# Running sum of the convolution in a PSUM bank, low parts of the projection weights on GpSimd

## The chip, the cores and the metric

One core of one Trainium2 chip runs the program. The metric is the time of one execution on the device in microseconds (us), median over runs. The core has TensorE (PE in the profile; PEld is its weight load), VectorE (DVE), ScalarE (ACT), GpSimd (POOL) and SyncE (SP), which issues the DMAs here. Each engine takes its instructions from its own queue, strictly in order.

## The reference, cut to what matters

One decoder layer over 1024 tokens and 1024 features:

```
u    = rmsnorm(x, norm_g) * (1 + scale) + shift        # scale, shift, gate from c
proj = u @ w_in                                        # 1024 -> 7168 columns
a    = conv_a * sigmoid(conv_bp)
a    = causal_depthwise_conv(a, conv_w, conv_b)        # 31 taps per channel
a    = silu(layernorm(a)) @ conv_pw
y_conv = a * silu(conv_gate)
r    = retention(rotary(q), rotary(k), v)              # 4 heads, in chunks
y_ret  = head_groupnorm(r) * silu(ret_gate)
h    = x + gate * (concat(y_conv, y_ret) @ w_out)
out  = rmsnorm(h, final_g)
```

## The kernel before, in words

Every big product is made three times over, to keep float32 precision: each operand is split into a high part (`hi`, a cast on ScalarE) and a low part (`lo`, the operand minus its high part, a subtraction on VectorE), and `mm3` (L70) adds hi·hi, hi·lo and lo·hi in PSUM.

A **unit** (L75) is 128 columns of a weight matrix times the resident 1024 x 1024 operand: two PSUM tiles of 128 x 512 (`ps[0]`, `ps[1]`, one bank each), for each of eight k three matmuls into `ps[0]` and three into `ps[1]`, 48 in all. `load_w` (L61) fetches a unit's weights (128 x 1024), casts the high part on ScalarE and makes the low part on VectorE; `raw`, `hi` and `lo` have two buffers each. The PSUM tiles of the units come from the pool `mm` with four banks (L48), so that two units can be in PSUM at once. The other four banks belong to the head of the kernel, later to the retention (`tr`, `sp`, `op`, `up`), at the end to the layer norm.

The stages, in order of time:

1. The head (until about 65 us): x is normalised and turned, `u` is built k by k, and four units (`EARLY`) run along with it.
2. Projection, convolution and retention (until about 700 us). `conv_pair(m)` (L250) makes a tile of 128 channels: a unit whose result goes through a sigmoid, a second unit whose PSUM result VectorE multiplies by it into the tile `a` (L260; 30 zero columns, set by GpSimd at L256, stand ahead of it). There are two buffers for `a`: pair m can write its `a` only once the taps of pair m - 2 are done. `conv_taps` (L233) then makes 31 taps on VectorE over 128 x 1024, each adding into the SBUF tile `y`, and adds `y` to `ysum` (L244). The taps have a priority 3000 below the rest, so they fill the time that VectorE has left. For each of four heads: `rotary` twice for q and k (units read out of PSUM by ScalarE, or twice by VectorE, L322 and L324), `values` (L329, weights of two `load_w` at once), two gate units, and `retention` in four chunks, in which GpSimd makes a power (`pow`, L422) for the group norm. `conv_pair` and `conv_gate` stand between these.
3. From `ysum` a matmul makes the mean (`mu`, L496); the layer norm of the convolution, the last gates, the output projection of the retention half, the pointwise convolution, the output projection of the convolution half and the final norm follow, with the low parts on VectorE through `split` (L57).

The order of the instructions in each engine's queue isn't written out by hand: a scheduler lays the program out on a timeline of its own, taking at each step the ready instruction of the highest priority, and that order is then fixed.

Of the kernel before, what the change touches and what calls it, by code (L numbers as in the profile page):

```python
# [12 lines left out]
P = 128  # L13
S = 1024
# [10 lines left out]
HALF = 512  # L25
EARLY = (8, 0, 9, 1)  # the units that run while u is built

# columns of the packed per-channel vectors
V_C, V_SH, V_SC, V_NG, V_CB, V_LG, V_LB, V_GG, V_GB, V_CW = 0, 8, 16, 24, 32, 40, 48, 56, 64, 72
V_N = V_CW + KT * CW  # L30
# columns of the packed decay constants
K_G, K_G2, K_KD = 0, 2 * H, 4 * H
# [6 lines left out]
def hybrid_layer(ctx: ExitStack, tc: tile.TileContext, x, vec, c_row, ada_ss, ada_g, adab_g, w_e, w_m, w_v,  # L39
# [7 lines left out]
    dram = ctx.enter_context(tc.tile_pool(name="dram", bufs=1, space=bass.MemoryType.DRAM))  # L47
    mmp = ctx.enter_context(tc.tile_pool(name="mm", bufs=4, space=bass.MemoryType.PSUM))  # L48

# [5 lines left out]

# [1 line left out]
    def split(hi, lo, src):  # L57
        nc.scalar.copy(hi, src)  # L58
        nc.vector.tensor_tensor(lo, src, hi.bitcast(F32), op=SUB)  # L59

    def load_w(src, shape, name, pool=None):  # L61
        raw = wpool.tile(shape, F32, tag="raw", name=f"raw_{name}")
        nc.sync.dma_start(raw, src)
        pool = pool or wpool
        hi = pool.tile(shape, F32R, tag="hi", name=f"hi_{name}", bufs=2)
        lo = pool.tile(shape, F32R, tag="lo", name=f"lo_{name}", bufs=2)
        split(hi, lo, raw)
        return hi, lo
# [6 lines left out]
    def unit(wh, wl, rh, rl, name, halves_first=False, pool=None, tag="mm"):  # L75
        """[128 columns of w]^T times the resident operand, both halves of its free axis."""
        ps = [(pool or mmp).tile([P, HALF], F32, tag=tag, name=f"ps_{name}_{i}") for i in range(2)]
        order = [(k, i) for k in range(KT) for i in range(2)]
        if halves_first:
            order.sort(key=lambda o: o[1])  # L80
        for k, i in order:
            sl = slice(i * HALF, (i + 1) * HALF)
            mm3(ps[i], wh[:, k], wl[:, k], rh[k][:, sl], rl[k][:, sl], k == 0, k == KT - 1)
        return ps

# [1 line left out]
    vec_t = const.tile([P, V_N], F32, name="vec_t")  # L87
# [11 lines left out]
    def col(base, k):  # L99
        return vec_t[:, base + k:base + k + 1]  # L100

    def bcast_rsqrt(pool, psp, sums, scale, n, rb):
        """sums: [128, n] column sums (token t = 128 j + partition); rb: PSUM [128, 128 n] gets rsqrt in every row."""
        v = pool.tile([P, n], F32, tag="rs_v", name="rs_v")
        nc.vector.tensor_scalar(v, sums, scale, EPS, op0=MUL, op1=ADD)
        r = pool.tile([P, n], F32, tag="rs_r", name="rs_r")
        nc.gpsimd.tensor_tensor(r, v, mhalf[:, :n], op=ALU.pow)
        for j in range(n):
            dg = pool.tile([P, P], F32, tag="rs_d", name="rs_d", bufs=4)
            nc.vector.tensor_scalar(dg, ident_t, r[:, j:j + 1], None, op0=MUL)  # L110
            nc.tensor.matmul(rb[:, j * P:(j + 1) * P], ones_t, dg, start=True, stop=True)

# [1 line left out]
    xts = [big.tile([P, D], F32, tag="big", name=f"xt{t}", bufs=17) for t in range(TT)]  # L114
# [10 lines left out]
    def head():  # L125
        """Builds u tile by tile and runs the first four units along with it, k on the outside."""
        xs = hp.tile([P, KT, S], F32, name="xs")
# [25 lines left out]
        def norm(t, xt_):  # L153
            """x / rms(x) of 128 tokens, turned so that features are on partitions."""
            ms = hp.tile([P, 1], F32, tag="ms", name=f"ms{t}", bufs=3)
            nc.scalar.activation(junk2, xt_, AF.Square, scale=D ** -0.5, accum_out=ms)
            nc.gpsimd.tensor_scalar(ms, ms, EPS, None, op0=ADD)
            nc.gpsimd.tensor_tensor(ms, ms, mhalf[:, 0:1], op=ALU.pow)
            nc.vector.tensor_scalar(xt_, xt_, ms, None, op0=MUL)
            for q in range(2):  # L160
                tp = hps.tile([P, 4, P], F32, tag=("paa", "pbb", "pcc", "pdd")[(2 * t + q) % 4], name=f"xp{t}{q}")
                for j in range(4):
                    k = 4 * q + j
                    nc.tensor.transpose(tp[:, j], xt_[:, k * P:(k + 1) * P], ident_t)
                dst = xs[:, 4 * q:4 * q + 4, t * P:(t + 1) * P]
                if q == 0 and t < 7:
                    nc.scalar.copy(dst, tp)
                else:
                    nc.vector.tensor_copy(dst, tp)
# [42 lines left out]
        make_u(0, halves(1))  # L212
        ps = [[mmp.tile([P, HALF], F32, tag="mm", name=f"ps_e{n}{i}") for i in range(2)] for n in range(2)]
        ps += [[hps.tile([P, HALF], F32, tag=t, name=f"ps_{t}") for t in u] for u in (("pcc", "pbb"), ("paa", "pdd"))]
# [18 lines left out]
    def conv_taps(m, ap):  # L233
        """Convolves one tile of channels; fills whatever time the vector engine has left."""
        with tc.high_priority(offset=-TAPS_LATER):
            y = convp.tile([P, S], F32, tag="y", name=f"y{m}")
            nc.vector.tensor_scalar(y, ap[:, 0:S], col(V_CW, m * CW), col(V_CB, m), op0=MUL, op1=ADD)
            for j in range(1, CW):
                nc.vector.scalar_tensor_tensor(y, ap[:, j:j + S], col(V_CW, m * CW + j), y, op0=MUL, op1=ADD)  # L239
            nc.sync.dma_start(d_y[m], y)  # L240
            if m == 0:
                nc.vector.tensor_copy(ysum, y)
            else:
                nc.vector.tensor_tensor(ysum, ysum, y, op=ADD)  # L244

    def in_unit(n):
        wh, wl = load_w(w_m[n - sum(e < n for e in EARLY)], [P, KT, P], f"w{n}")
        return unit(wh, wl, uh, ul, f"w{n}")
# [29 lines left out]
    def out_gate():  # L278
        """One step towards the residual's gate, the same in every partition."""
        k = len(gate_steps)  # L280
# [20 lines left out]

# [1 line left out]
    with tc.tile_pool(name="ret", bufs=1, reuse_waits="tile") as rp, \  # L303
# [25 lines left out]
        def values(h):  # L329
            vt = rp.tile([P, TT, 2 * P], F32, tag="v", name=f"v{h}")  # L330
            ws = [load_w(w_v[h, g], [P, 4, 2 * P], f"v{h}{g}") for g in range(2)]
            for tg in range(2):
                ps = [mmp.tile([P, 2, 2 * P], F32, tag="mm", name=f"ps_v{h}{tg}{i}") for i in range(2)]
                for k in range(KT):
                    wh, wl = ws[k // 4]
                    for j in range(4):
                        sl = slice((4 * tg + j) * P, (4 * tg + j + 1) * P)
                        mm3(ps[j // 2][:, j % 2], uh[k][:, sl], ul[k][:, sl], wh[:, k % 4], wl[:, k % 4],
                            k == 0 and j % 2 == 0, k == KT - 1 and j % 2 == 1)
                for i in range(2):  # L340
                    nc.scalar.copy(vt[:, 4 * tg + 2 * i:4 * tg + 2 * i + 2], ps[i])
            return vt

        def retention(h, q, k, v, sg):
            state = st_h = st_l = None
            for c in range(NCH):
# [10 lines left out]
                if c < NCH - 1:  # L357
                    # keys with tokens on partitions, decayed to the chunk's end
                    kth = rp.tile([P, 2, 2 * P], F32R, tag="kth", name=f"kth{n}")
# [12 lines left out]

                # scores, transposed: keys on partitions
                sp = rps.tile([P, 3 * P], F32, tag="sp", name=f"sp{n}")
# [10 lines left out]

                # outputs, tokens on partitions
                op = rps.tile([P, 2, 2 * P], F32, tag="op", name=f"op{n}")
# [23 lines left out]

                # group norm over the head's 256 values
                st6 = rp.tile([P, 2, 6], F32, tag="st6", name=f"st6{n}", bufs=2)
# [62 lines left out]
        negmu = f2.tile([P, S], F32, tag="y1", name="negmu")  # L476
        # layer norm, channels on partitions; what fits in before u is gone comes first
        def ln_center(m, tmp):
# [22 lines left out]

# [1 line left out]
    with tc.tile_pool(name="fin", bufs=1, reuse_waits="tile") as fp, \  # L503
# [62 lines left out]

# [1 line left out]
        for m in range(KT):  # L568
# [14 lines left out]

# [1 line left out]
        for t in range(TT):  # L585
# [48 lines left out]
def _layout(inp):  # L634
# [27 lines left out]

    # tables that depend on the shapes alone
    f4 = np.float32
# [52 lines left out]
```

## Time and profile before

| | |
|---|---|
| time, median of 2 runs | 1003.42 us (1003.21 to 1003.64) |
| span of the profiled execution | 1001.6 us |
| PE busy | 987.8 us, 99% |
| DVE busy | 739.3 us, 74% |
| ACT busy | 312.8 us, 31% |
| POOL busy | 35.9 us, 4% |

The span runs from the first to the last instruction of the profiled execution; the time of this execution itself isn't given apart from the two runs, which lie 1.6 to 2.0 us above the span. A busy time is what the engine worked; matmuls are pipelined, so a busy PE is not PE at its peak.

### The profile page before, as it was taken

How to read it: one execution, taken by the hardware profiler on the slowest of the kernel's cores; microseconds unless marked ns; L12 is line 12 of the kernel's file. 1: busy time of each engine (PE TensorE's matmuls, PEld its weight loads, DVE VectorE, ACT ScalarE, POOL GpSimd, SP SyncE). 2: the span in 40 equal slices, each digit the busy share in tenths (PEclk: the TensorE clock that was granted, in tenths of full speed). 3: DMA queues.
4: the chain of work that ended last, by engine and by line, in shares of the span. 5: the costliest groups of instructions: out<-in, count | busy, mean ns of one | idle time of the engine just before them, and what ended most of it. 6: DMA issues, size and time to landing. Idle time of an engine off the chain costs nothing.

```text
span 1001.6 us, 12564 instructions
## 1 busy us (share of the span) xinstructions
PE 987.8 (99%) x5108; PEld 843.6 (84%) x5108; DVE 739.3 (74%) x969; ACT 312.8 (31%) x489; POOL 35.9 (4%) x55
## 2 busy tenths in 40 slices
PE   7999999999999999999999999999999999999997
PEld 5888899888898888899888898888888888888886
DVE  6959999899998999999967679764446963442342
ACT  7831223332213322223233412443422711111221
POOL 2000000000000000100000000000000000000000
PEclk9999999999999999999999999999999999999999
DMA  9641111111132211113221022411784356541322
GB/s 351 236 168 43 43 43 64 63 64 43 64 106 74 74 63 63 43 64 127 63 84 42 25 103 63 147 64 64 264 277 152 127 172 209 187 137 63 127 95 84
DMA packets 40253, 108.80 MB, mean 109 GB/s; under 512 B 3458, under 2 KB 16002, under 8 KB 39043
## 3 DMA queue, kind: packets, MB, share of 16 engines
q1 hardware_dynamic: 40050, 107.74, 31.5%
q8 instruction: 40, 0.66, 0.3%
q10 hardware_dynamic: 144, 0.26, 0.1%
q14 instruction: 19, 0.15, 0.0%
HBM read 84.92 MB, written 23.07 MB: 108 GB/s over the span
## 4 chain that ended last, share of the span: by engine, by line
PE 96%; DVE 1%; DMA 1%; ACT 0%; issue 0%; SPq 0%; POOL 0%; POOLq 0%; DVEq 0%; ACTq 0%
PE ps_w L73 16%; PE ps_w L71 16%; PE ps_w L72 16%; PE ps_v L71 3%; PE ps_v L73 3%; PE ps_v L72 3%; PE ps_oc L73 3%; PE ps_or L72 3%; PE ps_oc L72 3%; PE ps_oc L71 3%; PE ps_or L73 3%; PE ps_pw L73 3%; PE ps_pw L71 3%; PE ps_or L71 3%; PE ps_pw L72 3%; PE op L73 1%
## 5 line engine op out<-in xcount | busy, mean ns | idle before, releaser
L239 DVE SCALAR_TENSOR_TENSOR y<-a,vec_t,y 128x1024 f32<-128x1024 f32 x240 | 300.5, 1278 | 1.3
L72 PE MATMUL ps_w<-ul,hi_w 128*128 128x512 f32 x704 | 275.2, 391 | 0.0
L73 PE MATMUL ps_w<-uh,lo_w 128*128 128x512 f32 x704 | 274.8, 391 | 0.0
L71 PE MATMUL ps_w<-uh,hi_w 128*128 128x512 f32 x704 | 274.6, 391 | 0.0
L72 PEld LDWEIGHTS ps_w<-ul,hi_w 128*128 128x128 f32 x704 | 132.3, 188 | 26.2 <-issue 0.2
L71 PEld LDWEIGHTS ps_w<-uh,hi_w 128*128 128x128 f32 x704 | 132.3, 188 | 25.9 <-issue 0.2
L73 PEld LDWEIGHTS ps_w<-uh,lo_w 128*128 128x128 f32 x704 | 132.2, 188 | 25.7
L72 PE MATMUL ps_v<-lo_v,uh 128*128 128x256 f32 x256 | 72.1, 283 | 0.0
L73 PE MATMUL ps_v<-hi_v,ul 128*128 128x256 f32 x256 | 71.8, 283 | 0.0
L71 PE MATMUL ps_v<-hi_v,uh 128*128 128x256 f32 x256 | 71.7, 283 | 0.0
L59 DVE TENSOR_TENSOR lo_w<-raw_w,hi_w 128x1024 fp32r<-128x1024 f32 x44 | 53.7, 1220 | 23.2 <-ACT hi_w L58 23.1
L58 ACT CAST hi_w<-raw_w 128x1024 fp32r<-128x1024 f32 x44 | 46.2, 1049 | 69.8 <-PE ps_w L72 27.5
L72 PE MATMUL ps_oc<-wol,ych 128*128 128x512 f32 (+1 forms) x136 | 51.2, 377 | 0.0
L73 PE MATMUL ps_oc<-woh,ycl 128*128 128x512 f32 (+1 forms) x136 | 51.2, 376 | 0.0
L71 PE MATMUL ps_oc<-woh,ych 128*128 128x512 f32 (+1 forms) x136 | 51.2, 376 | 0.0
L71 PE MATMUL ps_pw<-zh,hi_pw 128*128 128x512 f32 x128 | 49.8, 389 | 0.0
L72 PE MATMUL ps_pw<-zl,hi_pw 128*128 128x512 f32 x128 | 49.8, 389 | 0.0
L73 PE MATMUL ps_pw<-zh,lo_pw 128*128 128x512 f32 x128 | 49.8, 389 | 0.0
L72 PE MATMUL ps_or<-wol,hi_yr 128*128 128x512 f32 x128 | 49.8, 390 | 0.0
L73 PE MATMUL ps_or<-woh,lo_yr 128*128 128x512 f32 x128 | 49.6, 390 | 0.0
L71 PE MATMUL ps_or<-woh,hi_yr 128*128 128x512 f32 x128 | 49.4, 390 | 0.0
L72 PEld LDWEIGHTS ps_v<-lo_v,uh 128*128 128x128 f32 x256 | 49.0, 192 | 0.2
(219 smaller groups left out, 1552.4 us busy)
## 6 DMA issues: line engine op xcount, KB each, us to landing
raw_w<-w_m SPq DMA_DIRECT2D x44, 512.0 KB, 3.5
xt<-x SPq DMA_DIRECT2D x16, 512.0 KB, 4.5
aw<-ada_ss SPq DMA_DIRECT2D x8, 1024.0 KB, 6.7
wo<-w_out SPq DMA_DIRECT2D x16, 512.0 KB, 5.4
raw_v<-w_v SPq DMA_DIRECT2D x8, 512.0 KB, 3.5
d_y<-y SPq DMA_DIRECT2D x8, 512.0 KB, 2.9
ag<-ada_g SPq DMA_DIRECT2D x8, 512.0 KB, 3.5
d_yr<-sg SPq DMA_DIRECT2D x8, 512.0 KB, 2.8
```

The source lines that it names most:

```text
L58: nc.scalar.copy(hi, src)
L59: nc.vector.tensor_tensor(lo, src, hi.bitcast(F32), op=SUB)
L71: nc.tensor.matmul(ps, lh, rh, start=start, stop=False)
L72: nc.tensor.matmul(ps, lh, rl, start=False, stop=False)
L73: nc.tensor.matmul(ps, ll, rh, start=False, stop=stop)
L239: nc.vector.scalar_tensor_tensor(y, ap[:, j:j + S], col(V_CW, m * CW + j), y, op0=MUL, op1=ADD)
```

## The change

- The pool `mm` has three PSUM banks in place of four. The fourth is a pool of its own, `yps`, with one bank.
- `conv_taps` works in halves of 512 columns. The taps of a half add into the PSUM bank `yp`; ScalarE then copies it to `y` in SBUF, and VectorE adds it to `ysum`.
- `load_w` can make the low part on another engine. `in_unit` and `values` name GpSimd; the weights of the later stages (`yr`, `pw`) stay on VectorE.
- In the head the last of the tiles `ps_e` takes the bank of `yps`.

Lines that only delete comments are left out:

```diff
...
-    mmp = ctx.enter_context(tc.tile_pool(name="mm", bufs=4, space=bass.MemoryType.PSUM))
+    mmp = ctx.enter_context(tc.tile_pool(name="mm", bufs=3, space=bass.MemoryType.PSUM))
+    yps = ctx.enter_context(tc.tile_pool(name="yps", bufs=1, space=bass.MemoryType.PSUM))
...
-    def load_w(src, shape, name, pool=None):
+    def load_w(src, shape, name, pool=None, eng=None):
...
-        split(hi, lo, raw)
+        nc.scalar.copy(hi, raw)
+        (eng or nc.vector).tensor_tensor(lo, raw, hi.bitcast(F32), op=SUB)
         return hi, lo
...
-        ps = [[mmp.tile([P, HALF], F32, tag="mm", name=f"ps_e{n}{i}") for i in range(2)] for n in range(2)]
+        ps = [[mmp.tile([P, HALF], F32, tag="mm", name=f"ps_e{n}{i}") if n + i < 2 else
+               yps.tile([P, HALF], F32, tag="y", name="ps_e11") for i in range(2)] for n in range(2)]
...
             y = convp.tile([P, S], F32, tag="y", name=f"y{m}")
-            nc.vector.tensor_scalar(y, ap[:, 0:S], col(V_CW, m * CW), col(V_CB, m), op0=MUL, op1=ADD)
-            for j in range(1, CW):
-                nc.vector.scalar_tensor_tensor(y, ap[:, j:j + S], col(V_CW, m * CW + j), y, op0=MUL, op1=ADD)
+            for i in range(2):
+                o = i * HALF
+                sl = slice(o, o + HALF)
+                yp = yps.tile([P, HALF], F32, tag="y", name=f"yp{m}{i}")
+                nc.vector.tensor_scalar(yp, ap[:, o:o + HALF], col(V_CW, m * CW), col(V_CB, m), op0=MUL, op1=ADD)
+                for j in range(1, CW):
+                    nc.vector.scalar_tensor_tensor(yp, ap[:, o + j:o + j + HALF], col(V_CW, m * CW + j), yp,
+                                                   op0=MUL, op1=ADD)
+                nc.scalar.copy(y[:, sl], yp)
+                if m == 0:
+                    nc.vector.tensor_copy(ysum[:, sl], yp)
+                else:
+                    nc.vector.tensor_tensor(ysum[:, sl], ysum[:, sl], yp, op=ADD)
             nc.sync.dma_start(d_y[m], y)
-            if m == 0:
-                nc.vector.tensor_copy(ysum, y)
-            else:
-                nc.vector.tensor_tensor(ysum, ysum, y, op=ADD)
...
-        wh, wl = load_w(w_m[n - sum(e < n for e in EARLY)], [P, KT, P], f"w{n}")
+        wh, wl = load_w(w_m[n - sum(e < n for e in EARLY)], [P, KT, P], f"w{n}", eng=nc.gpsimd)
...
-            ws = [load_w(w_v[h, g], [P, 4, 2 * P], f"v{h}{g}") for g in range(2)]
+            ws = [load_w(w_v[h, g], [P, 4, 2 * P], f"v{h}{g}", eng=nc.gpsimd) for g in range(2)]
...
```

## Rows read from the trace of the kernel before

**Rows 1.** Page: busy time of each engine; chain that ended last, by engine.

```profile
PE 987.8 (99%) x5108; PEld 843.6 (84%) x5108; DVE 739.3 (74%) x969; ACT 312.8 (31%) x489; POOL 35.9 (4%) x55
...
PE 96%; DVE 1%; DMA 1%; ACT 0%; issue 0%; SPq 0%; POOL 0%; POOLq 0%; DVEq 0%; ACTq 0%
```

**Rows 2.** Busy time by stretch: stretch, its length, then each engine's busy us.

```profile
0.00:65.00 65.00, 57.58 (x265) 45.88 (x266) 46.23 (x71) 46.41 (x71) 7.41 (x22) 1.00 0.74 275
...
100.00:500.00 400.00, 400.00 (x2234) 349.62 (x2234) 377.34 (x458) 109.88 (x174) 15.06 (x14) 1.00 0.20 66
...
700.00:988.00 288.00, 288.00 (x1290) 239.04 (x1289) 139.71 (x185) 77.27 (x113) 5.87 (x9) 1.00 0.49 162
988.00:1001.60 13.60, 7.18 (x55) 6.74 (x53) 3.47 (x8) 2.46 (x7) 0.74 (x2) 0.95 0.20 77
```

**Rows 3.** Timeline of VectorE: start, us; runs of taps, PSUM reads of a rotary unit.

```profile
72.80 8.45 DVE L239 SCALAR_TENSOR_TENSOR y<-a,vec_t,y 128x1024 f32<-128x1024 f32 x7
...
90.56 0.68 DVE L322 TENSOR_TENSOR rb_q<-ps_w,cs_t 128x512 f32<-128x512 f32 x1
91.16 0.68 DVE L324 TENSOR_TENSOR rd_q<-ps_w,cs_t 128x512 f32<-128x512 f32 x1
...
586.37 9.21 DVE L239 SCALAR_TENSOR_TENSOR y<-a,vec_t,y 128x1024 f32<-128x1024 f32 x7
```

**Rows 4.** Groups of VectorE from 66 to 286 us (count, busy us, mean ns, idle before).

```profile
L239 DVE SCALAR_TENSOR_TENSOR y<-a,vec_t,y 128x1024 f32<-128x1024 f32 x105 | 130.3, 1276 | 0.1
L59 DVE TENSOR_TENSOR lo_w<-raw_w,hi_w 128x1024 fp32r<-128x1024 f32 x15 | 18.2, 1214 | 1.4 <-ACT hi_w L58 1.4
L59 DVE TENSOR_TENSOR lo_v<-raw_v,hi_v 128x1024 fp32r<-128x1024 f32 x3 | 3.7, 1221 | 0.7 <-ACT hi_v L58 0.7
```

**Rows 5.** The same groups from 66 to 647 us.

```profile
L239 DVE SCALAR_TENSOR_TENSOR y<-a,vec_t,y 128x1024 f32<-128x1024 f32 x240 | 300.5, 1278 | 1.3
L59 DVE TENSOR_TENSOR lo_w<-raw_w,hi_w 128x1024 fp32r<-128x1024 f32 x38 | 46.3, 1219 | 9.7 <-ACT hi_w L58 9.6
```

**Rows 6.** Groups of the whole span: a PSUM input against SBUF inputs alone.

```profile
L548 DVE TENSOR_TENSOR g<-ps_or,gacc 128x512 f32<-128x512 f32 x16 | 10.7, 685 | 9.4 <-PE ps_or L73 9.4
L549 DVE TENSOR_TENSOR xt<-xt,g 128x512 f32<-128x512 f32 x16 | 10.6, 683 | 0.2 <-DMA xt<-x 0.2
```

**Rows 7.** Groups of ScalarE: a PSUM half copied, a weight tile cast.

```profile
L58 ACT CAST hi_w<-raw_w 128x1024 fp32r<-128x1024 f32 x44 | 46.2, 1049 | 69.8 <-PE ps_w L72 27.5 <-issue 23.7 <-PE ps_v L73 13.7
...
L341 ACT COPY v<-ps_v 128x512 f32<-128x512 f32 x16 | 9.4, 586 | 47.5 <-PE ps_v L73 46.9
```

**Rows 8.** Timeline of GpSimd: start, us, line.

```profile
283.29 0.12 POOL L256 MEMSET a<- 128x30 f32 x1 [29.38 <-DVE y L239]
...
409.19 2.67 POOL L422 TENSOR_TENSOR rs<-rs,mhalf 128x2 f32<-128x2 f32 x1 [25.56 <-DVE rs L421]
...
520.94 0.69 POOL L422 TENSOR_TENSOR rs<-rs,mhalf 128x2 f32<-128x2 f32 x1 [13.18 <-DVE rs L421]
```

**Rows 9.** Timeline of VectorE: `a` of pairs 2 and 4 is written.

```profile
175.46 1.28 DVE L260 TENSOR_TENSOR a<-ps_w,sig 128x512 f32<-128x512 f32 x2
...
286.23 0.69 DVE L260 TENSOR_TENSOR a<-ps_w,sig 128x512 f32<-128x512 f32 x1 [0.67 <-PE ps_w L73]
```

**Rows 10.** Busy time of VectorE alone in two stretches, up to `a` and `mu`.

```profile
66.00:286.00 220.00, 211.20 (x252) 1.00 0.17 60
...
66.00:647.00 581.00, 519.91 (x646) 1.00 0.20 68
```

**Rows 11.** The matmul `mu`: duration ns min/median/max, first and last start.

```profile
L496 PE MATMUL mu<-ysum,ones_t x4: 590/592/594, 646.8 to 648.1; 128*128 128x512 f32 x4
```

**Rows 12.** Timeline: a low part on VectorE, and TensorE where it is used.

```profile
134.02 1.23 DVE L59 TENSOR_TENSOR lo_v<-raw_v,hi_v 128x1024 fp32r<-128x1024 f32 x1 [0.65 <-ACT hi_v L58]
...
138.67 0.40 PE L71 MATMUL ps_v<-hi_v,uh 128*128 128x256 f32 x2
...
139.84 0.28 PE L72 MATMUL ps_v<-lo_v,uh 128*128 128x256 f32 x1
```

## The prediction

> **What bounds the kernel now.** I read the page first: TensorE is busy 987.8 of 1001.6 us, and the chain that ended last runs over it for 96% of the span [rows 1]. Then the busy time by stretch: in the first 65 us TensorE lacks 7.4 us, in the last 13.6 us it lacks 6.4, and in between it lacks nothing; the stretches from 100 to 500 and from 700 to 988 us are full to the last digit [rows 2]. So TensorE sets the time. The change leaves its matmuls as they are, touches neither the loads of the head nor the last tile's end, and 13.8 us is all that any change beside TensorE could give back. It can hardly make this kernel faster; the question is whether it opens gaps in TensorE. Third, VectorE: 377.3 of 400 us busy from 100 to 500 us [rows 2], because taps fill every gap. It is the engine that can get late, so I weigh what it gains and loses, and when its work is due.
>
> **The change part by part.**
>
> *Taps.* Seven taps take 8.45 us where those of two tiles alternate and 9.21 us where one tile is alone [rows 3]. With the last one's own length taken off (1.28 us), a tap starts every 1.195 or every 1.321 us: one that reads what the tap just ahead wrote costs 0.126 us more. A half: an operation on 512 columns starts 0.60 us after the one ahead [rows 3]; a tap takes some 0.06 us more than a subtraction of its size, since it multiplies by a column as well [rows 4]; so 0.66 us, and 0.786 behind its own predecessor. With one bank the halves go strictly one after another, so no second tile can alternate any more; only other work of VectorE between two taps hides the 0.126. Per tile: 30 taps cost 35.9 us now; 60 halves cost 39.6 us (all covered) to 47.2 us (none). I take 45.6: taps stand in runs, so I count four in five as uncovered. Reading PSUM costs nothing extra: 685 against 683 ns at one size [rows 6]. VectorE writing PSUM no row shows. I take nothing, as for the read; the bounds are 0.07 us a tap either way, 4 us a tile: 512 columns more cost 0.54 us (1.14 less 0.60), so 0.12 of a tap's 0.66 us is fixed, and I let half of it go or come again. The first tap and the addition to `ysum` cost about the same in halves as whole.
>
> *Bank waits.* The next half's first tap waits until ScalarE has copied the bank, 0.59 us [rows 7]; VectorE's own addition to `ysum` fills 0.6 us meanwhile, so 0 to 0.7 us, 16 times; I take 0.4. Behind the waiting tap stand the low parts of the retention and the reads of the units' banks, for which TensorE waits; behind the waiting copy stand the casts and ScalarE's reads of the banks. ScalarE's 9 us for 16 copies are hidden: it is busy 31% [rows 1].
>
> *Low parts.* VectorE loses 46 subtractions up to 647 us (38 and, for the four heads, 8 [rows 5]) of 1.14 us start to start (1.22 less the 0.08 by which such rows overlap [rows 3]), 52 us; six more come later. GpSimd gains them. What one costs there no row shows: from below 1.2 us as on VectorE, from above 4.2 us (30 columns in 0.12 us [rows 8], times 1024/30). I take the geometric middle, 2.2 us. Either end is on time: cast 1.05 [rows 7] and 4.2 us fit in the some 10.7 us of a unit of 48 matmuls (288 us for 1290 [rows 2]). The tightest case is the second weight tile of `values`: VectorE had its low part at 135.3 us, TensorE filled the time with other work and used it at 139.8 [rows 12]: 4.5 us to spare, and 4.2 - 1.2 = 3 of it are gone at worst. In GpSimd's queue a low part can stand behind the zeros of `a`, which wait for taps (29 us idle ahead of them [rows 8]), or behind a `pow`; both are laid out by when they are due. The `raw` buffer comes free a little later, so SP's next load starts later by as much; two buffers cover that.
>
> *The two engines at SBUF.* A `pow` of two columns takes 0.69 us where VectorE is little used and 2.67 us amid taps with two SBUF inputs [rows 8]: GpSimd waits for VectorE. Whether VectorE waits for GpSimd too, no row shows: between nothing and a whole low part (4.2 us) each. Taps in PSUM read one SBUF tile and need not collide; retention and rotary still read two. I take 0.5 us for each low part: half of 2.2 us, where it meets such an operation, one time in two.
>
> The Trainium skill (SBUF — State Buffer, Who interferes with whom) says that the port pair shared by VectorE and GpSimd is an exclusive lock, held for a whole instruction, against VectorE operations with two SBUF inputs. By it VectorE does wait, and the hold is more than nothing; its GPSIMD Engine Reference (Performance versus the Vector engine) gives 4497 ns for an addition of 2048 columns, so by estimate 2.25 us for 1024, and the sum would stay as it is.
>
> *Three banks.* The second tile of a unit needs the bank of the unit ahead's first tile, which is done 3 matmuls before that unit's end; 3 more, and the bank is wanted, 1.3 us later. VectorE needs 1.2 us for a rotary half's two reads, and stands in a tap of up to 0.8 us when it is due. But TensorE's queue is laid out around such waits: at 138.7 us it went on with other work until the low part came [rows 12], and here 21 matmuls of `ps[0]` are at hand. Cost: 0 to 1.2 us at each of 37 units that VectorE reads (8 rotary, 6 of pairs, 23 at the end), 0 to 44 us; I take 2.
>
> *When taps are due.* The tiles of pair 2 were read at 175.5 us [rows 9], though TensorE was in `values` by 138.7 [rows 12]: two of four banks were held for 37 us until `a` came free. With three banks one would be left, and TensorE would stop. But serial taps end tile 0 early: 105 taps in 220 us [rows 4] put 30 of them at 129 us, at the new cost and without low parts at some 135. Pair 4 needs tiles 0 to 2 by 286 us [rows 9]. VectorE has 220 us from 66 on; 211.2 busy [rows 10], of which 105 x 1.195 = 125.5 are taps and 18 x 1.14 = 20.5 low parts [rows 4], so 154.5 are to be had. Wanted: 3 x 45.6 + 18 x 0.5 + 6 x 0.4 = 148. For `mu` at 647 us [rows 11]: 581 - (519.9 - 286.8 - 52.4) = 400 [rows 5, 10]; wanted 8 x 45.6 + 23 + 6.4 = 394. Both are met, by 6 us. TensorE stays full.
>
> **Sum.** Span 1001.6 + 0 (TensorE's work) + 0 (taps, low parts, lock: within VectorE's room) + 2 (banks) = 1003.6; what lies around the span is 1.8 us by the median of the runs, 1003.42. Forecast **1005 us**.
>
> **The rivals.**
>
> 1. *Taps cost more, and VectorE becomes the bound (slower).* Place: `a` of pair 4, then `mu`. It decides once the taps of a tile cost over (154.5 - 11.4) / 3 = 47.7 us for pair 4, or (400 - 29.4) / 8 = 46.3 for `mu`. For it: the uncovered tap is at 47.2 already, and a slower write to PSUM adds up to 4. Against: VectorE has no other work that must come before, and the last gates can run ahead of `mu`. At 51 us a tile: late by 10 us for pair 4 and 38 for `mu`, of which the gates hide some; 1015 to 1042.
> 2. *Low parts hold VectorE (slower).* It decides, at taps of 45.6 us, once a low part holds VectorE for over 0.5 + 6/46 = 0.63 us. If each holds it for its full 2.2 us, 46 x 1.7 = 78 us more are wanted and 72 are missing at `mu`; gates hide up to half, so 1040 to 1075. For it: the `pow` that waited [rows 8]. Against: taps, more than half of VectorE's time, no longer read two SBUF tiles. This is what the skill's exclusive lock would do at its worst.
> 3. *Small gaps.* The orders are laid out for one course of time and the engines run in another; with one spare bank fewer and ScalarE, VectorE and GpSimd each waiting on the taps, a late engine shows in TensorE. Some ten of the 37 bank changes and some of the waits at 0.5 to 1.2 us: 1007 to 1023.
> 4. *It doesn't relieve VectorE.* The low parts go and longer taps come: 52 us against 8 x 9.7 = 78. VectorE is then no freer, but as long as TensorE is full the time is the forecast's. *Faster* would need TensorE's 7.4 us of the head, which nothing here feeds.
>
> **How the numbers follow.** Forecast, with rival 4 (1000 to 1007): 0.45. Rival 3: 0.31. Rival 1: 0.14. Rival 2: 0.09. Over 2% faster: 0.01. About 2% is what a measurement of this kernel can tell from no change; 2% slower is 1023.5. Rival 3 ends there, rival 1 begins below it with some 0.03 of its chance; so slower 0.20, same 0.79. The range takes the forecast and rival 3 whole and the lower part of rival 1: 1000 to 1030.
>
> **What would show it.** Right: PE has 0 idle from 65 to 988 us; taps at 0.66 to 0.79 us, 47 or less per tile; low parts of 1.2 to 4.2 us on POOL; VectorE busier from 500 to 650 us. Rivals 1 and 2: VectorE 99% busy to 640 us, PE waiting for `a` (L260) or `mu`; in 1 taps over 0.79 us, in 2 two-input operations of VectorE stretched beside low parts. Rival 3: PE idle in pieces of about 1 us at the first matmuls of `ps[1]`. I am wrong if writing PSUM from VectorE costs over 0.1 us a tap or if TensorE stops where pair 2 holds two banks.

## The result, and the profile after

The changed kernel takes 1017.8 us (median of 2 runs, 1016.46 to 1019.13) against 1003.42: ratio 1.0145, interval 1.0112 to 1.0177. The forecast was 1005, the range 1000 to 1030. The slowdown of 1.45% is clear of the spread of the runs, and under the 2% that the prediction took as the limit of what can be told. The span grew by 13.1 us, from 1001.6 to 1014.7.

The page of the changed kernel, busy times and chain [rows 1]:

```profile
PE 993.2 (98%) x5108; PEld 846.5 (83%) x5108; DVE 765.6 (75%) x1173; ACT 322.9 (32%) x505; POOL 159.7 (16%) x107
...
PE 94%; DVE 3%; issue 1%; ACT 1%; POOL 0%; POOLq 0%; DVEq 0%; ACTq 0%
```

TensorE still sets the time, but 3% of the chain now runs over VectorE. The busy times by stretch say where (columns as in [rows 2]):

```profile
100.00:500.00 400.00, 400.00 (x2235) 349.87 (x2234) 370.30 (x576) 117.74 (x187) 89.82 (x46) 1.00 0.19 65
500.00:640.00 140.00, 140.00 (x793) 122.07 (x791) 128.88 (x201) 43.46 (x70) 28.99 (x15) 1.00 0.20 68
640.00:650.00 10.00, 8.94 (x43) 6.77 (x43) 9.65 (x21) 4.52 (x9) 2.93 (x2) 1.00 0.10 41
650.00:660.00 10.00, 6.62 (x46) 5.38 (x44) 9.78 (x23) 4.16 (x9) 1.20 (x2) 0.96 0.20 68
660.00:670.00 10.00, 7.95 (x42) 7.16 (x43) 9.90 (x22) 3.23 (x7) 0.00 (x0) 0.70 0.00 0
670.00:675.00 5.00, 3.75 (x19) 2.52 (x18) 4.62 (x12) 3.62 (x7) 0.70 (x1) 1.00 0.39 126
675.00:1001.00 326.00, 326.00 (x1469) 270.83 (x1468) 150.04 (x202) 90.69 (x132) 17.61 (x14) 1.00 0.46 155
```

TensorE is full up to 640 us and from 675 us on. All that was lost lies between: 7.7 of 35 us idle (35 less 8.94, 6.62, 7.95 and 3.75); the other 5.4 us of the 13.1 are in busy time, since matmuls that come singly or at a lower clock count as busy for longer (0.41 us each at 662 us, 0.28 at 651). The timeline of TensorE in that stretch (start, length; in brackets the idle time before, and who ended it):

```profile
646.63 1.02 PE L505 MATMUL mu<-ysum,ones_t 128*128 128x512 f32 x2
648.70 0.89 PE L439 MATMUL tp<-ident_t,rn 128*128 128x128 f32 x4 [1.04 <-ACT rn L437]
...
660.98 1.15 PE L439 MATMUL tp<-ident_t,rn 128*128 128x128 f32 x4 [2.17 <-ACT rn L437]
...
662.35 0.41 PE L75 MATMUL op<-vch,sl 128*128 128x256 f32 x1
662.56 0.41 PE L73 MATMUL op<-vch,sh 128*128 128x256 f32 x1
...
673.27 1.13 PE L505 MATMUL mu<-ysum,ones_t 128*128 128x512 f32 x2
673.83 0.79 PE L73 MATMUL ps_w<-uh,hi_w 128*128 128x512 f32 x1
```

Half of `mu` ran at 646.6 us, as before [rows 11]; the other half came 26.6 us later, and the first matmul of the next gate stands right behind it. Between the two TensorE had the retention of head 3 alone, a chain of short steps through ScalarE and VectorE. What the second half of `mu` waits for is in VectorE's timeline:

```profile
636.88 3.12 DVE L246 SCALAR_TENSOR_TENSOR yp<-a,vec_t,yp 128x512 f32<-128x512 f32 x4
...
641.17 0.75 DVE L246 SCALAR_TENSOR_TENSOR yp<-a,vec_t,yp 128x512 f32<-128x512 f32 x1
641.83 0.55 DVE L390 TENSOR_TENSOR sm<-sp,mask_t 128x384 f32<-128x384 f32 x1
...
672.53 0.68 DVE L252 TENSOR_TENSOR ysum<-ysum,yp 128x512 f32<-128x512 f32 x1
```

The first half's bank isn't free in between either. ScalarE reads both halves of `mu` into `negmu` only after 675 us, though the first was done at 647.7:

```profile
675.29 1.09 ACT L506 ACTIVATE negmu<-mu 128x512 f32<-128x512 f32 x2 [0.54 <-DMA d_y<-y]
```

The pool of `negmu` is opened where that of the convolution is closed (L482, L483 of the changed kernel), and the last wait ahead of this reading is ended by the store of `y`. In the kernel before, the same reading began at 648.6 us.

The last addition to `ysum` ends at 673.2 us; in the kernel before it began at 638.3 us and took 1.22. Four taps in a run start 0.79 us apart ((3.12 - 0.75) / 3); a tap with another operation behind it hands over after 0.66 (641.83 - 641.17).

VectorE's groups from 66 to 673 us, with what is new, and what was stretched:

```profile
L246 DVE SCALAR_TENSOR_TENSOR yp<-a,vec_t,yp 128x512 f32<-128x512 f32 x480 | 361.3, 753 | 11.2
L444 DVE TENSOR_TENSOR sg<-sg,yn 128x256 f32<-128x256 f32 x28 | 13.2, 494 | 3.6 <-ACT yn L442 3.6
L244 DVE TENSOR_SCALAR yp<-a,vec_t 128x512 f32<-128x512 f32 x16 | 13.0, 811 | 0.3
L325 DVE TENSOR_TENSOR k<-x_k,cs_t 128x1024 f32<-128x1024 f32 x4 | 11.7, 2929 | 0.7 <-ACT x_k L324 0.6
L325 DVE TENSOR_TENSOR q<-x_q,cs_t 128x1024 f32<-128x1024 f32 x4 | 10.3, 2575 | 0.2 <-ACT x_q L324 0.2
L252 DVE TENSOR_TENSOR ysum<-ysum,yp 128x512 f32<-128x512 f32 x14 | 9.6, 683 | 8.7 <-ACT y L248 8.7
L334 DVE TENSOR_TENSOR q<-q,rb_q 128x512 f32<-128x512 f32 x8 | 9.0, 1127 | 0.0
```

The two rotary products of L325 took 1217 and 1220 ns in the kernel before, where they are L316; with the low parts on GpSimd they take 2929 and 2575 in the mean:

```profile
L316 DVE TENSOR_TENSOR q<-x_q,cs_t 128x1024 f32<-128x1024 f32 x4 | 4.9, 1220 | 0.0
L316 DVE TENSOR_TENSOR k<-x_k,cs_t 128x1024 f32<-128x1024 f32 x4 | 4.9, 1217 | 0.0
```

A low part takes 2438 ns on GpSimd in the mean (the page):

```profile
L69 POOL TENSOR_TENSOR lo_w<-raw_w,hi_w 128x1024 fp32r<-128x1024 f32 x44 | 107.3, 2438 | 384.4 <-ACT hi_w L68 374.6
```

### The profile page after: what moved, and what is told of

Its sections match the earlier page's. It is cut to its first block, busy times and chain, and to the rows that moved or that the text cites. A ratio compares the mean times of both kernels' runs of the same rounds, so it can differ in the third digit from the quotient of the medians.

```text
span 1014.7 us, 12815 instructions
## 1 busy us (share of the span) xinstructions
PE 993.2 (98%) x5108; PEld 846.5 (83%) x5108; DVE 765.6 (75%) x1173; ACT 322.9 (32%) x505; POOL 159.7 (16%) x107
## 4 chain that ended last, share of the span: by engine, by line
PE 94%; DVE 3%; issue 1%; ACT 1%; POOL 0%; POOLq 0%; DVEq 0%; ACTq 0%
PE ps_w L73 16%; PE ps_w L74 16%; PE ps_w L75 16%; PE ps_v L74 3%; PE ps_v L75 3%; PE ps_v L73 3%; PE ps_or L75 3%; PE ps_oc L75 3%; PE ps_oc L73 3%; PE ps_oc L74 3%; PE ps_or L73 3%; PE ps_pw L73 3%; PE ps_pw L75 3%; PE ps_or L74 3%; PE ps_pw L74 3%
## 5 line engine op out<-in xcount | busy, mean ns | idle before, releaser
L246 DVE SCALAR_TENSOR_TENSOR yp<-a,vec_t,yp 128x512 f32<-128x512 f32 x480 | 361.3, 753 | 11.2
L69 POOL TENSOR_TENSOR lo_w<-raw_w,hi_w 128x1024 fp32r<-128x1024 f32 x44 | 107.3, 2438 | 384.4 <-ACT hi_w L68 374.6
L74 PEld LDWEIGHTS ps_w<-ul,hi_w 128*128 128x128 f32 x704 | 132.3, 188 | 26.6 <-issue 0.5
L60 DVE TENSOR_TENSOR wol<-wo,woh 128x1024 fp32r<-128x1024 f32 x16 | 20.0, 1268 | 44.8 <-ACT woh L59 44.8
L73 PEld LDWEIGHTS ps_v<-hi_v,uh 128*128 128x128 f32 x256 | 49.1, 192 | 0.2
```

The source lines that it names most:

```text
L69: (eng or nc.vector).tensor_tensor(lo, raw, hi.bitcast(F32), op=SUB)
L73: nc.tensor.matmul(ps, lh, rh, start=start, stop=False)
L74: nc.tensor.matmul(ps, lh, rl, start=False, stop=False)
L246: nc.vector.scalar_tensor_tensor(yp, ap[:, o + j:o + j + HALF], col(V_CW, m * CW + j), yp, op0=MUL, op1=ADD)
```

## The experiments

After the result two questions were open: why a late `ysum` costs TensorE anything, with six gates still to be made, and why `ysum` is late. For the first, theory M says that the gates stand behind `mu` in the program's order, theory B that `mu`'s two tiles take two of the units' three banks, so that no gate, which needs two, can run. Theory L answers the second: the low parts on GpSimd hold VectorE, so that an operation with two SBUF inputs takes longer.

**1. Three gates ahead of `mu`** (changed kernel).

```diff
-        for m in range(1, 2):
+        for m in range(1, 5):
             conv_gate(m)
...
-        for m in range(2, KT):
+        for m in range(5, KT):
             conv_gate(m)
```

> The changed kernel with gates 2 to 4 ahead of the mean mu in the program's order. Theory M (TensorE loses its 13 us only between the two halves of mu, 646.6 to 673.8 us, because the sum ysum is 34 us later than before and the gates stand behind mu): the gates fill that stretch, TensorE has no idle from 65 us to the end, 1002 to 1006 us. Theory B (with three banks the two tiles of mu leave the units too few banks): mu still takes two of three when it comes, so the gap moves and stays, 1011 to 1018 us. Theory L (low parts on GpSimd hold VectorE, which delays TensorE all along): VectorE is as slow as before, but little waits for it; 1005 to 1018 us.

Measured: 1003.86 us, ratio 1.0004 to the kernel before (0.9995 to 1.0014). The whole loss is gone, with the same VectorE (480 taps, 361.3 us) and a `ysum` whose last addition starts at 669.1 us. `mu` in this kernel (minimum, median, maximum, first and last start):

```profile
L505 PE MATMUL mu<-ysum,ones_t x4: 590/592/594, 692.4 to 696.2; 128*128 128x512 f32 x4
```

So lateness as such costs nothing when gates are there to be run. M foresaw this. B had expected 1011 to 1018 us, with the gap moved and not gone, and missed: with three gates ahead of it `mu` comes at 692.4 us, 23 us after `ysum` is complete, and doesn't wait for it any more. This run alone speaks for M; the next one decides.

**2. `mu` in the sum's bank** (changed kernel). The program's order stays; only the bank is another.

```diff
-            mu = mmp.tile([P, HALF], F32, tag="mm", name=f"mu{i}")
+            mu = yps.tile([P, HALF], F32, tag="y", name=f"mu{i}")
```

> The changed kernel with the two tiles of mu in the bank of the running sum instead of the units' banks. Theory B: the gates have three banks and run ahead of mu, 1002 to 1007 us. Theory M, if the gates stand behind mu by the order of the program and not for want of a bank: the gap stays, 1014 to 1020 us. Theory L: 1014 to 1020 us.

Measured: 1003.85 us, ratio 1.0005 (0.9996 to 1.0014). Its busy times by stretch:

```profile
640.00:660.00 20.00, 20.00 (x103) 16.98 (x103) 18.84 (x41) 6.20 (x11) 3.10 (x2) 1.00 0.14 54
660.00:680.00 20.00, 20.00 (x113) 17.14 (x112) 12.49 (x24) 10.69 (x19) 5.49 (x3) 1.00 0.53 188
```

The last addition to `ysum` starts at 668.9 us and `mu` runs from 675.0 to 680.2 us, yet TensorE is full. With the units' banks free of `mu`, the scheduler lays gates ahead of it although the program names `mu` first. So the program's order need not change: M, which expected 1014 to 1020 us, falls, and B holds. The edit also keeps the first half of `mu` from running early (675.0 us in place of 646.6), so it shows that the loss hangs on the banks that `mu` holds, and not which of its halves, or the late reading into `negmu`, counts for how much. In the changed kernel the next gate's first matmul starts at 673.83 us, before `mu` is read at 675.29: so one bank was free for a gate and, by count, the second was wanting.

**3. The same edit on the kernel before**, three gates ahead of `mu`, as a control.

> Edit: the kernel before with the gates of tiles 2 to 4 laid out ahead of mu, as in the experiment on the changed kernel that took its time to 1003.9 us. Control. Theory: before has nothing to gain there, since its mu finds TensorE full: 1002.5 to 1004.5 us. Rival (laying the gates ahead of mu is worth something by itself): 990 to 1000 us, and then the changed kernel with this edit would still be 1% behind.

Measured: 1003.48 us, ratio 1.0 (0.999 to 1.0009). The order is worth nothing by itself; in experiment 1 it gave back what the change had taken, no more.

**4. The PSUM sum alone** (changed kernel, low parts on VectorE).

```diff
-        wh, wl = load_w(w_m[n - sum(e < n for e in EARLY)], [P, KT, P], f"w{n}", eng=nc.gpsimd)
+        wh, wl = load_w(w_m[n - sum(e < n for e in EARLY)], [P, KT, P], f"w{n}")
...
-            ws = [load_w(w_v[h, g], [P, 4, 2 * P], f"v{h}{g}", eng=nc.gpsimd) for g in range(2)]
+            ws = [load_w(w_v[h, g], [P, 4, 2 * P], f"v{h}{g}") for g in range(2)]
```

> The changed kernel with the low parts back on VectorE. VectorE loses the holds by GpSimd (23 us by the rows of the changed kernel) and gets 46 subtractions of 1.14 us, 52 us, up to mu. Theory M: mu comes some 29 us later still, near 700 us, and pairs 4 and 6 get late as well; 1035 to 1060 us. Theory L (the holds are the cause): 1003 to 1012 us.

Measured: 1062.09 us, ratio 1.0586 (1.057 to 1.0601), 2 us above what M expected. L, read as the whole cause, had 1003 to 1012 us and fell: a hold costs VectorE less (0.5 us) than making the low part itself (1.14). L325 is back at 1218 ns: the stretching belongs to the low parts on GpSimd. TensorE's timeline:

```profile
693.48 2.08 PE L505 MATMUL mu<-ysum,ones_t 128*128 128x512 f32 x2 [3.64 <-DVE ysum L252]
...
720.12 2.07 PE L505 MATMUL mu<-ysum,ones_t 128*128 128x512 f32 x2 [23.71 <-DVE ysum L252]
```

`ysum` is complete at about 720 us, 47 later than in the changed kernel. 46 low parts of 1.14 us come back to VectorE (52 us) and some 23 us of holds go; VectorE's idle time up to then, added up from its timeline, is 44 us against 31 us. That is 29 + 13 = 42 of the 47; the rest isn't accounted for.

**5. The low parts on GpSimd alone** (kernel before: taps in SBUF, four banks).

```diff
-        split(hi, lo, raw)
+        nc.scalar.copy(hi, raw)
+        (eng or nc.vector).tensor_tensor(lo, raw, hi.bitcast(F32), op=SUB)
...
+        wh, wl = load_w(w_m[n - sum(e < n for e in EARLY)], [P, KT, P], f"w{n}", eng=nc.gpsimd)
...
+            ws = [load_w(w_v[h, g], [P, 4, 2 * P], f"v{h}{g}", eng=nc.gpsimd) for g in range(2)]
```

> The kernel before with the low parts on GpSimd alone: taps in SBUF, two tiles in turn, four banks. Theory M: VectorE gains 52 us and loses the holds, and taps keep their 1.2 us, so ysum is ready before 638 us and TensorE stays full, 1001 to 1005 us; low parts take longer than 2.4 us, since the taps read two SBUF tiles. Theory L: every low part meets a tap, holds of 1 to 2.4 us for 46 of them, 46 to 110 us against the 52 gained; 1003 to 1040 us, with taps of over 2 us in the trace.

Measured: 1042.4 us, ratio 1.0392 (1.0341 to 1.0443). The four runs lie between 1037.9 and 1048.1 us, and the trace is of the longest. M (1001 to 1005 us) falls; the range of L ended 2 us below, at 1040. The taps and low parts, all of the span, then by minimum, median and maximum:

```profile
L240 DVE SCALAR_TENSOR_TENSOR y<-a,vec_t,y 128x1024 f32<-128x1024 f32 x240 | 356.7, 1500 | 3.8
L68 POOL TENSOR_TENSOR lo_w<-raw_w,hi_w 128x1024 fp32r<-128x1024 f32 x44 | 122.2, 2778 | 359.8 <-ACT hi_w L67 356.6 <-PE ps_w L74 3.2
```

```profile
L240 DVE SCALAR_TENSOR_TENSOR y<-a,vec_t,y x240: 1246/1284/3485, 67.8 to 675.7; 128x1024 f32<-128x1024 f32 x120
L68 POOL TENSOR_TENSOR lo_v<-raw_v,hi_v x8: 2393/2547/18444, 126.4 to 626.0; 128x1024 fp32r<-128x1024 f32 x8
```

A tap takes 1500 ns in the mean in place of 1278 [rows 5]: 240 x 0.22 = 53 us, as much as the 52 us that VectorE gave away. The median is 1284 ns: 27 of the 240 taps take over 2 us, as L expected, and the others are as before. GpSimd waits as well. One low part took 18.4 us beside a run of 17 taps, which start 1.2 us apart as ever, and TensorE waited for it (timelines of VectorE and GpSimd; list of waits):

```profile
132.95 20.41 DVE L240 SCALAR_TENSOR_TENSOR y<-a,vec_t,y 128x1024 f32<-128x1024 f32 x17
137.11 18.44 POOL L68 TENSOR_TENSOR lo_v<-raw_v,hi_v 128x1024 fp32r<-128x1024 f32 x1 [8.23 <-ACT hi_v L67]
```

```profile
PE ps_v L73 <- POOL lo_v L68: 13.5, 1, 13.5
```

In all TensorE is idle for 27 us between 100 and 500 us here.

The two parts of the change need each other. Each alone costs 4 to 6%; together they cost 1.45%.

**6. Low parts made twice** (changed kernel). The second copy is work that nothing needs.

```diff
-        (eng or nc.vector).tensor_tensor(lo, raw, hi.bitcast(F32), op=SUB)
+        for _ in range(2 if eng else 1):
+            (eng or nc.vector).tensor_tensor(lo, raw, hi.bitcast(F32), op=SUB)
```

> Edit: the changed kernel, where GpSimd makes each of its low parts twice over, so that the second copy is work that nothing needs. Theory L (a low part on GpSimd holds VectorE by about 0.5 us, through its operations with two SBUF inputs, and that is part of why ysum is late): 46 more low parts, about 23 us more hold by 673 us; ysum, last added at 672.5 us in the changed kernel, would come at about 695, and TensorE, which has nothing left but the retention of head 3, would lose about all of it: 1030 to 1045 us. Rival (the holds are harmless, the lateness is that of the serial taps alone): ysum stays at 670 to 676 us and the time at 1016 to 1021 us, since GpSimd is only 16% busy.

Measured: 1046.07 us, ratio 1.0426 (1.0411 to 1.0442), 28 us above the changed kernel. The last addition to `ysum` starts at 699.1 us, 26.6 later, for 46 more low parts: 0.58 us for each. The rival (670 to 676 us, 1016 to 1021) falls; L holds, 4 us later at `ysum` and 1 us longer than it expected. Part of the time is lost elsewhere: TensorE is idle for 12 us between 100 and 500 us, where the changed kernel has no gap. TensorE's timeline at the most costly place:

```profile
429.87 0.39 PE L76 MATMUL ps_w<-uh,lo_w 128*128 128x512 f32 x1
437.22 0.80 PE L74 MATMUL ps_w<-uh,hi_w 128*128 128x512 f32 x1 [6.96 <-DVE rd_k L334]
437.81 0.63 PE L75 MATMUL ps_w<-ul,hi_w 128*128 128x512 f32 x1
```

A unit stands 7 us for a bank that VectorE's rotary reads too late.

**7. Low parts made twice, and `mu` in the sum's bank** (the edits of 6 and 2).

> Edit: as the kernel with each low part made twice, and besides the two mu tiles take the bank of the convolution's sum in place of two of the three banks of the units. Theory B (a late ysum costs time only because mu holds two of the three banks that the gates need): ysum as late as in the kernel with low parts made twice (about 695 us), but the gates run ahead of mu and hide it: 1003 to 1009 us. Rival (ysum's lateness costs by itself, or the holds open gaps elsewhere): within 10 us of the kernel with low parts made twice, 1025 to 1045 us.

Measured: 1025.33 us, ratio 1.022 (1.0203 to 1.0237): 20.7 us less than experiment 6, but 16 above what theory B allowed. The rival's range (1025 to 1045) just holds it, and of its two reasons the second, gaps that the holds open elsewhere. Its busy times by stretch:

```profile
400.00:500.00 100.00, 93.04 (x514) 81.21 (x513) 92.74 (x129) 23.58 (x36) 38.61 (x19) 0.97 0.18 64
...
640.00:660.00 20.00, 20.00 (x100) 16.43 (x99) 18.81 (x30) 6.92 (x11) 9.90 (x4) 1.00 0.10 30
660.00:680.00 20.00, 20.00 (x111) 17.26 (x110) 19.71 (x35) 5.18 (x9) 6.50 (x4) 1.00 0.29 103
680.00:700.00 20.00, 20.00 (x107) 16.82 (x107) 16.21 (x34) 9.93 (x19) 5.49 (x3) 1.00 0.43 158
```

At `mu` B is right: TensorE is full from 640 to 700 us with a `ysum` as late as 693 us. The 22 us that stay lie before: over the stretches from 100 to 640 us TensorE is idle for 15 us, 7 of them at the unit of experiment 6, after which its matmuls run at a lower clock for a while (0.97 in the mean from 400 to 500 us). So holds of 23 us leave TensorE full until 640 us and holds of twice that don't; the margin lay between. Against experiment 2, from which it differs by the second copies alone, the last addition to `ysum` starts 23.9 us later, 0.52 us for each:

```profile
L252 DVE TENSOR_TENSOR ysum<-ysum,yp x14: 675/686/689, 170.7 to 668.9; 128x512 f32<-128x512 f32 x14
...
L253 DVE TENSOR_TENSOR ysum<-ysum,yp x14: 672/687/689, 173.8 to 692.8; 128x512 f32<-128x512 f32 x14
```

**8. Halves alternating** (changed kernel). The first half of a tile adds up in the PSUM bank, the second in SBUF, tap by tap in turn, so that no tap reads what the one just ahead wrote.

```diff
-            for i in range(2):
-                yp = yps.tile([P, HALF], F32, tag="y", name=f"yp{m}{i}")
...
+            yp = yps.tile([P, HALF], F32, tag="y", name=f"yp{m}")
+            acc = (yp, y[:, HALF:S])
+            for j in range(CW):
+                for i in range(2):
+                    src, wj = ap[:, i * HALF + j:i * HALF + j + HALF], col(V_CW, m * CW + j)
...
+                        nc.vector.scalar_tensor_tensor(acc[i], src, wj, acc[i], op0=MUL, op1=ADD)
```

> Edit: the changed kernel, but only the first half of a tile adds up in the PSUM bank; the second adds up in SBUF, and the taps of the two halves alternate. Theory of the serial taps (a tap that reads what the one just ahead wrote costs 0.126 us more): taps start about 0.66 us apart instead of 0.786, the 480 of them lose about 55 us, ysum is ready before 647 us and the time is 1002 to 1006 us, with taps of 0.66 to 0.70 us. Rival (collision at SBUF: the half that adds in SBUF reads two SBUF tiles, as in the kernel before with the low parts on GpSimd, where the tap's mean rose from 1278 to 1500 ns): its taps are stretched to 0.8 us or more in the mean, low parts on GpSimd take over 2.6 us, ysum is not earlier than 665 us and the time is 1012 to 1030 us.

Measured: 1033.35 us, ratio 1.0298 (1.0283 to 1.0313). The taps from 66 to 700 us, by half:

```profile
L248 DVE SCALAR_TENSOR_TENSOR y<-a,vec_t,y 128x512 f32<-128x512 f32 x240 | 221.1, 930 | 0.0
L248 DVE SCALAR_TENSOR_TENSOR yp<-a,vec_t,yp 128x512 f32<-128x512 f32 x240 | 179.2, 747 | 0.4
```

The same operation beside the same low parts: 747 ns with its sum in PSUM, 930 with its sum in SBUF. The view by tile shows that this is not the write to SBUF (minimum, median, maximum):

```profile
L248 DVE SCALAR_TENSOR_TENSOR y<-a,vec_t,y x240: 718/743/2893, 69.4 to 662.5; 128x512 f32<-128x512 f32 x120
L246 DVE TENSOR_SCALAR y<-a,vec_t x8: 535/540/2237, 67.7 to 613.9; 128x512 f32<-128x512 f32 x8
```

Of the 240 taps into SBUF 212 take under 0.8 us. The other 28 take over 1 us, up to 2893 ns; each of them overlaps in time with a low part on GpSimd, and together they add 45 us. The theory of the serial taps was right on its own point: where the taps of the two halves alternate, one starts 0.66 us after the other, against 0.79 in the changed kernel. But what that could bring, 0.13 us at the 305 taps that stand in runs, is 40 us, and the collisions took more. The rival was right on the mechanism: taps of 930 ns in the mean where it said 800 or more. Its other marks were just missed (low parts `lo_w` of 2568 ns where it said over 2600, the last addition to `ysum` at 664.3 us where it said not before 665), and the time is 3 us above its range, since TensorE loses time long before `mu`: it is idle for 14 us between 100 and 500 us.

Not tried: three banks for the units with the sum left in SBUF. What three banks cost by themselves is known only from the whole change: nothing until 640 us. Nor was a buffer for `negmu` tried that needn't wait for the store of `y`.

## Why the prediction was off

That 1017.8 us lies inside 1000 to 1030 is luck. The range was made so wide for rival 3, which didn't come, and for the lower part of rival 1, whose taps didn't cost more; the loss came at the place of rival 1 by another way.

**What held.** TensorE is full to 640 us and from 675 on; no gap opened at a unit's bank, so rival 3 fell and the 2 us of the sum for banks measured 0 there; and none opened at pair 2 or pair 4. Taps start 0.79 us apart behind their own predecessor (0.786 forecast), and writing PSUM costs nothing for them. Rival 4 was right too: VectorE isn't relieved, busy for 765.6 us against 739.3 [rows 1]. Of the signs, VectorE is busier from 500 to 650 us (138.5 us against 110.2), two-input operations are stretched as rival 2 said, and TensorE loses its time about `mu`; but VectorE is 93% busy from 66 to 640 us and not 99%. A low part takes 2.40 us in the median (2.2 taken). A hold was 0.5 us: from the means of the stretched groups, after less before, times their counts, L325 lost 12.3 us (4 x 1.71 + 4 x 1.36), L334 5.4, the splits of q, k and v 2.6, `sg` 2.1 and a small step of the norm 1.2, together 23.6 us, 0.51 for each of 46 low parts (0.52 by experiments 2 and 7). By the Trainium skill (SBUF — State Buffer, Who interferes with whom) a VectorE operation with two SBUF inputs and a GpSimd one that reads SBUF exclude each other for a whole instruction, and a VectorE operation with at most one SBUF input, outside the modes that use both port pairs, doesn't contend. Experiments 5 and 8 agree: 1500 ns against 1278, and 930 against 747.

**The step that failed** is "Both are met, by 6 us. TensorE stays full", at `mu`. By its own terms, with what was measured:

| term, up to `mu` | forecast, us | measured, us |
|---|---|---|
| taps, 8 tiles | 365 | 356 (305 x 0.79 + 175 x 0.66) |
| first taps, more than before | 0 | 6.5 (16 x 0.811 less 8 x 0.806) |
| additions to `ysum`, more than before | 0 | 1.8 (11.0 less 9.2) |
| bank waits | 6.4 | 8.7 |
| holds | 23 | 24 |
| wanted | 394 | 397 |
| VectorE's idle time not usable | 0 | 22 |
| room | 400 | 378 |

The 305 taps are those that have a tap right behind them in VectorE's timeline from 66 to 673 us. What was wanted came out right to 3 us, by errors that cancel. (The room for pair 4 is 154.8 by its own terms, not 154.5; nothing hangs on it.) The bank waits came out near although VectorE's addition to `ysum` doesn't fill the time of ScalarE's copy: in all 16 halves it starts after the copy has ended, and in six of them VectorE stands idle ahead of it, together for 8.7 us.

The room did not come out: the sum counted the whole of VectorE's 61 us of idle time [rows 10] as open to taps. In the changed kernel 31 us of it stay idle, 8.7 of them the bank waits. Taps weren't lacking there: from tile 1 on, `a` of a tile is written before the taps of the tile ahead have ended (that of tile 7 at 585 us; the taps of tile 6 ended at 600). VectorE takes its queue in a fixed order and stands idle ahead of an instruction whose input is late. For 16.5 us it did so within a half, with the next tap ready behind that instruction; for 12.9 us, the bank waits among them, where one half hands the bank to the next; shorter gaps make up the rest. The longest of the first kind:

```profile
307.44 3.13 DVE L246 SCALAR_TENSOR_TENSOR yp<-a,vec_t,yp 128x512 f32<-128x512 f32 x4
312.89 1.28 DVE L301 SCALAR_TENSOR_TENSOR gacc<-ag,cact,gacc 128x1024 f32<-128x1024 f32 x1 [2.32 <-DMA ag<-ada_g]
314.10 0.75 DVE L246 SCALAR_TENSOR_TENSOR yp<-a,vec_t,yp 128x512 f32<-128x512 f32 x1
```

397 less 378 says that 19 us of work were missing at 647 us; the timeline has 21 taps and an addition still to come at 646.6 us, some 16 us. VectorE needs 26 us for these, since the retention, of higher priority, goes in between.

**The second failure** is in rival 1, "the last gates can run ahead of `mu`". It named the place and gave the price as 1015 us at the least because gates would hide some; the price that came is near that by another way: taps were cheap (44.6 us a tile, under its 46.3), and the gates hid nothing. They could have hidden all (experiments 1 and 2). The part on three banks counted the banks of units behind units, and pair 2's; it left out `mu`'s two tiles, which come from the same pool. By count a gate fits beside them with four banks, and with three it doesn't. Shown: the bank (experiment 2 against the changed kernel, with 3 as the control) and the hold (6 against the changed kernel, 7 against 2). Only read from rows and not isolated by a run: how the lateness splits between idle time and first taps, and what the late reading into `negmu` adds.

No version beats the kernel before: with `mu` in the sum's bank TensorE is full again, and the time is the old one.

## What to carry to other kernels

Not all idle time of an engine is room for more work. With its queue in a fixed order it stands ahead of an instruction whose input is late, though ready work lies behind it: here VectorE kept 31 of its 61 us of idle time with taps still to be done all the while. When a pool loses a buffer, list every tile that comes from it, not only the loop's: the one long-lived tile that waits for a slow engine sets what can run ahead of it. Before work is moved from VectorE to GpSimd, count the SBUF inputs of VectorE's main loop: here a low part gave VectorE back 1.14 us and cost it 0.51 where the taps read one SBUF tile, and all of it where they read two (experiment 5).

## What the hardware showed that was not expected

- A first tap (one tensor input and per-channel constants) takes 0.81 us for 512 columns into PSUM, 0.54 for 512 into SBUF (experiment 8) and 0.806 for 1024 into SBUF in the kernel before. The tap with two tensor inputs shows no such difference (medians in experiment 8: 746 ns into PSUM, 743 into SBUF). The Trainium skill (VectorE: DVE Perf Modes, Why PSUM operands drop a tier) says that any PSUM operand keeps VectorE from its double rate for fp32; the rows agree, here for an output.
- The granted clock fell to 0.70 in the mean from 660 to 670 us, after TensorE had had gaps of 0.4 to 2.2 us from 652 us on. Its levels are 1.2 and 2.4 GHz; the matmuls of `op` came 0.21 us apart at the lower one and 0.12 at the higher (the same line at 651 us). In experiment 4, after 24 us of waiting, a matmul of `mu` took up to 1223 ns where 590 is usual.
